# A decoder block's output projection: eight block products with all weights from one matrix, or seven with sums of blocks

## The chip, the core and the metric

The kernel runs on one core of a Trainium2 chip. The metric is the device time of one execution in microseconds, as the median of several runs. The engines are TensorE (PE, matmuls into PSUM banks of 128 x 512 fp32), VectorE (DVE) and ScalarE (ACT) for element-wise work, GpSimd (POOL), and SyncE (SP), whose queue issues nearly all DMAs here.

## What is computed

One decoder layer on 1024 tokens of width 1024, all in fp32. Cut to the part that matters:

```python
y_b = c @ w_proj_conv[l]                              # the conv projection
g_a, g_b = jnp.split(jax.nn.sigmoid(g + gate_b[l]), 2, axis=-1)
x = x + (g_a * y_a + g_b * y_b) @ w_out[l]            # the output projection
h = rms_norm(x, ffn_norm_w[l])
gt, up = jnp.split(h @ w_gate_up[l], 2, axis=-1)
x = x + (jax.nn.silu(gt) * up) @ w_down[l]
```

`m = g_a * y_a + g_b * y_b` is the 1024 x 1024 left matrix of the output projection, `w_out` the 1024 x 1024 right one.

## The kernel before

Every fp32 operand of a matmul is split into a high part (a cast to fp32r, `split_hi`, ScalarE, L119) and a low part (the difference, `split_lo`, VectorE, L124); a product is then three matmuls, hi x hi, hi x lo, lo x hi (`mm3`, L167). A weight tile of 128 x 1024 comes through a stream (`Stream`, L338): `next()` hands out the oldest tile and first fetches ahead until three are under way (load by SP into one of two buffers `wraw`, cast to `whi`, subtraction to `wlo`, three buffers each).

**Order of the work.** The instructions are traced in the order of the text. A scheduler then orders them on each engine by when it expects them to be ready; `with after(ins)` (L135) puts what is traced inside behind `ins` on that engine's queue. Each queue then runs strictly in its order.

**LayerNorm of the conv branch** (`ln_chunks`, L1519) works in two halves of 512 tokens (sb) during the attention projection, from a pool `b1` (`bp`), and fills `cT_hi`, `cT_lo`. Its last part runs into the conv projection.

**Conv projection** (L1633 to L1645). For each of 8 column blocks c of 128 channels and each half sb: 24 matmuls into one of four PSUM banks (`gemm_T`), the gate loaded (`gated`, L1597, four buffers `gt`), `ya` loaded (L1640), then on VectorE a product (L1642) and a sum (L1643), which give the block (c, sb) of m transposed, and a split into `mT_hi`, `mT_lo`. The blocks go in the groups (0,1,2), (3,4), (5,6), (7).

**Output projection** (L1701 to L1724). m is the stationary operand, w_out the moving one, 512 columns wide. Three passes (`WO`, L440): columns 0 to 511 for all eight token tiles (eight banks), then columns 512 to 1023 for tokens 0 to 511 (four banks), then for tokens 512 to 1023 (four banks). Per pass eight inner blocks k; a weight tile holds two of them (`ld_pair`, L425). Behind the first weight load SP loads the eight row tiles of x into `xa` (L1711), in the room that b1 left. After a pass VectorE adds each bank to `xa` (L1720), SP stores it to `x2_d` (L1721), ScalarE takes the sum of squares (`squares`, L1665).

**The FFN's norm.** When both column halves of tokens 0 to 511 are done, `rows_of` (L1669) computes 1/rms in 15 tiny VectorE operations (L1671, L648 to L660), `norm2` (L1674) scales a row tile (L1678), transposes it on TensorE (L1681) and splits it into `h2_hi`, `h2_lo`. Tokens 0 to 511 are turned in the third pass behind k = 3 to 6, in four banks that the pass does not use. The FFN's first gate product (`gate(0, 0)`, L1743) follows at once and takes a bank of the tag "pg" of the pool `ps`.

**Seven block products.** The FFN already uses Winograd's form of a 2 x 2 block product with 7 instead of 8 products. `SEVEN` (L447) lists left side, right side, bank ("a", "b" or "c", four PSUM banks each), result block and whether it is then complete. Left sides S1 to S4 and right sides T1 to T4 are sums of blocks; a bank is added to the result after each of its products and goes on accumulating. `ld_seven` (L457) loads a left and a right side (256 KB each) per step, `weight_sums` (L507) makes T1 to T4 of a weight matrix from loaded rows and stores them to DRAM in pieces of 128 KB, `side_sums` (L535) makes S1 to S4. In the down projection (`seven`, L482) both sides come from DRAM.

Of the kernel before, what the change touches and what calls it, by code (L numbers as in the profile page):

```python
# [10 lines left out]
F32 = mybir.dt.float32  # L11
# [5 lines left out]
P = 128  # L17
S = 1024
# [39 lines left out]
def kernel(  # L58
# [329 lines left out]
    td = {z: [dr.tile([P, 512], F32, name=f"td{z}_{j}") for j in range(NFF // 2)] for z in SUMS}  # L388
    b_d = dr.tile([H, TL], F32, name="b_d")
# [35 lines left out]
    def ld_pair(w, k, c):  # L425


        def go():
            raw = wraw()
            nc.sync.dma_start(  # L430
                raw[:].rearrange("p (k c) -> p k c", c=512),
                w[k * P : (k + 2) * P, 512 * c : 512 * (c + 1)].rearrange("(k p) c -> p k c", p=P),
            )
            hi, lo = wsplit(raw)
            return hi[:].rearrange("p (k c) -> p k c", c=512), lo[:].rearrange("p (k c) -> p k c", c=512)

        return go


    WO = ((0, (0, 1)), (1, (0,)), (1, (1,)))  # L440
    for c, _ in WO:
        ws.plan([ld_pair(wout, k, c) for k in range(0, NKT, 2)])

# [10 lines left out]
    def ld_seven(n, sides, w, sums, raw_tile):  # L457
# [22 lines left out]
        return [step(a_, b_, j) for a_, b_, _, _, _ in SEVEN for j in range(n)]  # L480

    def seven(n, stream, bank, add, soon):  # L482

        o = {}
        for z, (_, _, s_, (l, c), full) in enumerate(SEVEN):
# [3 lines left out]
            for js in [[j] for j in range(n - 2)] + ([[n - 2, n - 1]] if z == 6 else [[n - 2], [n - 1]]):  # L489
# [4 lines left out]
                for i in range(4):  # L494
# [9 lines left out]
                    if js[-1] == n - 1:  # L504
                        add(l, i, c, o[s_][i], full)

# [997 lines left out]
    bp = b1.enter_context(tc.tile_pool(name="b1", bufs=2, reuse_waits="tile"))  # L1504

# [13 lines left out]
    def ln_chunks(sb):  # L1519
# [4 lines left out]
        def half(tag):  # L1524
            return bp.tile([P, 512], F32, tag=tag, name=nm("ln" + tag), bufs=2)
# [8 lines left out]
        s1h, s1l = [bp.tile([P, 512], F32R, tag="sq", name=nm(t_), bufs=2) for t_ in ("lnmh", "lnml")]  # L1534
# [37 lines left out]
    part = bp.tile([P, P], F32R, tag="part", name="part", bufs=1)  # L1572
    pool.memset(f32(part[:]), 1.0 / D)

# [21 lines left out]

    def gated(d, cs):  # L1597
        g = bp.tile([P, 512], F32, tag="gt", name=nm("gt"), bufs=4)
        nc.sync.dma_start(g[:], d[:, cs])
        act.activation(g[:], g[:], AF.Sigmoid)  # L1600
        return g
# [30 lines left out]
    mT_hi, mT_lo = [a_[:5] + b_ + a_[5:] for a_, b_ in zip(y_first("mT"), y_last("mT"))]  # L1632
    for cl in ((0, 1, 2), (3, 4), (5, 6), (7,)):  # L1633
        pair = [(c, ws.next()) for c in cl]
        for sb in range(2):
            cs = slice(sb * 512, (sb + 1) * 512)
            for c, w in pair:
# [6 lines left out]
                split_hi(mT_hi[c][:, cs], g[:])  # L1644
                split_lo(mT_lo[c][:, cs], g[:], mT_hi[c][:, cs])  # L1645
# [12 lines left out]
    h2_hi = big.tile([P, NKT, S], F32R, tag="xhi", name="h2_hi")  # L1658
    h2_lo = big.tile([P, NKT, S], F32R, tag="xlo", name="h2_lo")
# [29 lines left out]
    wo_banks = [(ps, "pm"), (ps, "pm"), (ps, "pg"), (ps, "pg")] + [(pw, "pw")] * 4  # L1689

    def wo_bank(t_):
        p_, tag = wo_banks[t_]
        return p_.tile([P, 512], F32, tag=tag, name=nm("wo"))

    ntr = [0]

    def tr_first():
        ntr[0] += 1
        return ps.tile([P, 512], F32, tag=("pm", "pg")[ntr[0] % 2], name=nm("tr"))

    r2 = [None, None]  # L1701
    for z, (c, ls) in enumerate(WO):
        ts_ = [4 * l + i for l in ls for i in range(4)]
        o = {t_: wo_bank(t_) for t_ in ts_}
        for k in range(NKT):
            if k % 2 == 0:
                whi, wlo = ws.next()
            if z == 0 and k == 0:
                with after(last_of(mybir.EngineType.SP)):
                    for i in range(NT):  # L1710
                        nc.sync.dma_start(xa[i][:], xs[i * P : (i + 1) * P, :])  # L1711
            for t_ in ts_:
                tk = slice(t_ * P, (t_ + 1) * P)
# [278 lines left out]
```

## Time and profile before

| | us |
|---|---|
| median of 3 runs (lowest, highest) | 1742.43 (1741.9, 1744.05) |
| the profiled execution | 1742.87 |
| its span in the trace | 1741.1 |
| conv projection, TensorE | about 920 to 1008.5 |
| output projection, TensorE | 1008.5 to 1099.2 |

A page of the profile gives each engine's busy time, and the chain of work that ended last, followed back from the end. "L120" is a line of the kernel. Timelines list instructions with start, duration, engine, operation, tiles out<-in, and in brackets the idle time of the engine before and what ended it. A matmul's duration in the trace is longer than the distance to the next one, since matmuls are pipelined.

### The profile page before, as it was taken

The numbers are of one execution on the slowest core, as the hardware profiler recorded it, in microseconds if no ns is written. First come the engines' busy times: TensorE is split into PE (matmuls) and PEld (weight loads), VectorE is DVE, ScalarE is ACT, GpSimd is POOL, SyncE is SP. The second block draws the span as 40 slices with busy tenths as digits, with TensorE's granted clock in tenths as the row PEclk, the third lists the DMA queues.
The fourth block names the chain that finished last, engine by engine and source line by source line (L and its number), as shares of the span: only waits on it lengthen the run. The fifth ranks groups of instructions, "written<-read, shape, count | busy, mean of one in ns | idle before, by whom it ended". The sixth has DMA issues, their size and how long they took to land.

```text
span 1741.1 us, 25854 instructions
## 1 busy us (share of the span) xinstructions
PE 1728.2 (99%) x9293; PEld 1488.6 (85%) x9293; DVE 1249.4 (72%) x2090; ACT 856.2 (49%) x1950; POOL 210.9 (12%) x199
## 2 busy tenths in 40 slices
PE   9999999999999999999999999999999999999999
PEld 7997889998998999988787888888888888888887
DVE  7575889898987988977787525876676666565554
ACT  5333435767776776756366313633333333333332
POOL 3997851000000000000000000000000000000000
PEclk9999999999999999999999999999999999999999
DMA  6343454234345244343863544235445444597663
GB/s 200 118 129 119 161 177 140 91 107 134 104 110 151 80 119 131 103 140 135 310 208 100 173 157 154 89 99 185 152 152 173 160 151 147 173 369 274 216 219 130
DMA packets 253253, 271.68 MB, mean 156 GB/s; under 512 B 15746, under 2 KB 177602, under 8 KB 253124
## 3 DMA queue, kind: packets, MB, share of 16 engines
q1 hardware_dynamic: 250848, 263.25, 46.7%
q0 software_dynamic: 1840, 5.19, 1.0%
q8 instruction: 73, 1.20, 0.3%
q10 hardware_dynamic: 436, 1.58, 0.2%
q14 instruction: 56, 0.46, 0.1%
HBM read 175.55 MB, written 78.16 MB: 146 GB/s over the span
## 4 chain that ended last, share of the span: by engine, by line
PE 91%; DVE 3%; DMA 2%; ACT 2%; POOL 1%; issue 1%; SPq 0%; POOLq 0%; DVEq 0%
PE acc L963 28%; PE acc L500 12%; PE pg L168 11%; PE pg L170 11%; PE pg L169 11%; PE sc L1272 2%; PE sc L1271 2%; PE pT L1310 2%; PE wo L170 2%; PE wo L169 2%; PE wo L168 2%; DVE acc L582 1%; PE pW L169 1%; PE pW L168 1%; PE pW L170 1%; PE pg L1089 1%
## 5 line engine op out<-in xcount | busy, mean ns | idle before, releaser
L582 DVE SCALAR_TENSOR_TENSOR acc<-u,cw,acc 128x1023 f32<-128x1023 f32 (+14 forms) x240 | 303.5, 1265 | 14.4 <-ACT acc L576 11.9
L168 PE MATMUL pg<-whi,hT_hi 128*128 128x256 f32 x704 | 200.2, 286 | 0.5 <-DVE v L125 0.5
L170 PE MATMUL pg<-whi,hT_lo 128*128 128x256 f32 x704 | 200.1, 285 | 0.0
L169 PE MATMUL pg<-wlo,hT_hi 128*128 128x256 f32 x704 | 199.7, 284 | 0.0
L120 ACT CAST whi<-wraw 128x1024 fp32r<-128x1024 f32 x100 | 105.0, 1052 | 126.4 <-PE wo L170 48.2
L125 DVE TENSOR_TENSOR wlo<-draw,whi 128x1024 fp32r<-128x1024 f32 x75 | 91.8, 1224 | 86.1 <-ACT whi L120 84.4
L125 DVE TENSOR_TENSOR wlo<-wraw,whi 128x1024 fp32r<-128x1024 f32 x85 | 104.9, 1236 | 56.5 <-ACT whi L120 55.9
L120 ACT CAST whi<-draw 128x1024 fp32r<-128x1024 f32 x75 | 79.0, 1053 | 129.6 <-PE acc L500 116.1
L168 PEld LDWEIGHTS pg<-whi,hT_hi 128*128 128x128 f32 x704 | 134.1, 191 | 2.2 <-DVE v L125 0.7
L169 PEld LDWEIGHTS pg<-wlo,hT_hi 128*128 128x128 f32 x704 | 134.4, 191 | 1.9
L170 PEld LDWEIGHTS pg<-whi,hT_lo 128*128 128x128 f32 x704 | 134.3, 191 | 1.7
L500 PE MATMUL acc<-wlo,whi 128*128 128x512 f32 x308 | 120.0, 390 | 0.0
L500 PE MATMUL acc<-whi,wlo 128*128 128x512 f32 x308 | 119.9, 389 | 0.0
L168 PE MATMUL pg<-hT_hi,whi 128*128 128x512 f32 x288 | 114.7, 398 | 0.1
L169 PE MATMUL pg<-hT_lo,whi 128*128 128x512 f32 x288 | 114.2, 397 | 0.0
L170 PE MATMUL pg<-hT_hi,wlo 128*128 128x512 f32 x288 | 113.8, 395 | 0.0
L1278 ACT ACTIVATE E<-E,mn 128x640 f32<-128x640 f32 (+7 forms) x128 | 99.7, 779 | 27.1 <-DVE mn L1273 26.4
L120 ACT CAST whi<-s 128x1024 fp32r<-128x1024 f32 x54 | 56.9, 1053 | 107.3 <-PE acc L963 103.5
L963 PE MATMUL acc<-h_hi,whi 128*128 128x512 f32 x240 | 93.5, 390 | 0.0
L963 PE MATMUL acc<-h_lo,whi 128*128 128x512 f32 x240 | 93.5, 390 | 0.0
L1273 DVE CUSTOM_DVE_ANT_0 E<-sc,tb 128x512 f32<-128x512 f32 (+3 forms) x128 | 74.1, 585 | 26.9 <-PE pT L1310 13.1
L963 PE MATMUL acc<-h_hi,wlo 128*128 128x512 f32 x240 | 90.2, 390 | 0.0
(337 smaller groups left out, 4554.9 us busy)
## 6 DMA issues: line engine op xcount, KB each, us to landing
wraw<-in_w_gate_up_dram SPq DMA_DIRECT2D x44, 512.0 KB, 4.9
wraw<-in_w_in_dram SPq DMA_DIRECT2D x40, 512.0 KB, 4.6
qs<-qs SPq DMA_DIRECT2D x96, 128.0 KB, 2.3
wd<-in_w_down_dram SPq DMA_DIRECT2D x44, 256.0 KB, 3.1
tdT<-wd SPq DMA_DIRECT2D x88, 128.0 KB, 4.7
draw<-sdS SPq DMA_DIRECT2D x44, 256.0 KB, 3.7
draw<-tdT SPq DMA_DIRECT2D x44, 256.0 KB, 4.0
wraw<-in_w_in_dram SPq DMA_DIRECT2D x32, 256.0 KB, 3.3
```

The lines of the kernel that those rows point to most:

```text
L120: act.copy(dst, src)
L125: last_lo[0] = dve.tensor_tensor(dst, src, f32(hi), op=ALU.subtract).ins
L168: pe.matmul(o, lh, rh, start=start, stop=False)
L169: pe.matmul(o, lh, rl, start=False, stop=False)
L170: last_mm[0] = pe.matmul(o, ll, rh, start=False, stop=stop).ins
L500: m = pe.matmul(o[s_][i][:], l_[:, ts], r_[:, 512:], start=start and j + y_ == 0, stop=j == n - 1 and y_ == 2, skip_group_check=not start,)
L582: dve.scalar_tensor_tensor(a_, us[c][:, : S - n], cw[:, c, t : t + 1], a_, op0=ALU.mult, op1=ALU.add)
L963: last_mm[0] = pe.matmul(o[:], a_[x_][:, k, :], b_[y_][:, k, :], start=start and k + x_ + y_ == 0, stop=k == 3 and x_ == 1, skip_group_che ...
L1271: pe.matmul(o[:, :w], qh[:, qs], k, start=True, stop=False)
L1272: last_mm[0] = pe.matmul(o[:, :w], ql[:, qs], k, start=False, stop=True).ins
L1273: dve.tensor_tensor_reduce(e[:, ks], o[:, :w], tb[:, S - nk + c0 : S - nk + c0 + w], 1.0, mn[:, j : j + 1] if c0 else 3.0e38, ALU.add, ALU ...
L1278: act.activation(e[:, :nk], e[:, :nk], AF.Exp, bias=mn[:, j : j + 1], scale=-1.0, accum_out=l[:, j : j + 1])
```

## The change

The output projection becomes seven block products. m is cut into 2 x 2 blocks of 512 tokens x 512 channels, where the channel blocks are those of even and odd c, so that a pair (c - 1, c) gives one piece of every block; w_out is cut likewise, its row tiles into even and odd ones.

- Right sums: `weight_sums` of w_out, 8 chunks, one after every second of the 16 turns of the conv projection, queued behind VectorE's last instruction there; stored to `to` in DRAM.
- Left sums: after both halves of a pair, `side_sums` makes S1 to S4 from the four unsplit blocks and stores them to `so`. The unsplit blocks stay in `gt` buffers until then; a second set of four buffers is added in a pool `bs`, in the room of the LayerNorm's tiles, which get a pool of their own that closes before the conv projection.
- The left blocks 11, 12 and 22 are read from `mT_hi`, `mT_lo` in place; for even c the second token half is no longer split.
- Order of the products (`WSEVEN`): 11 (bank b), 12 (a), S2 (b), S1 (c), S4 (c), S3 (b), 22 (b). Weight steps: two tiles of two pairs for 11, 12 and 22 (`ld_two`), four tiles (left | right) for each S.
- Loads of S2, S1 and S4 with their right sides go into 12 rooms of 128 x 1024, in the place of `cT_hi` and half of `cT_lo`; SP gets them in one block behind the last load: S2, four row tiles of x, S1, four row tiles of x, S4. S3 goes through the two `wraw` buffers.
- After each product VectorE adds its four banks to `xa`, complete or not. The transposes of `norm2` take the banks of a and c; they are traced behind step 3 of S3 and steps 0 to 2 of 22.

```diff
+    so = {z: [dr.tile([P, 512], F32, name=f"so{z}_{j}") for j in range(NKT // 2)] for z in SIDES[3:]}
+    to = {z: [dr.tile([P, 512], F32, name=f"to{z}_{j}") for j in range(NKT // 2)] for z in SUMS}
...
-    for c, _ in WO:
-        ws.plan([ld_pair(wout, k, c) for k in range(0, NKT, 2)])
+    WSEVEN = tuple(SEVEN[z] for z in (0, 1, 2, 3, 5, 4, 6))
...
+    for e_ in WSEVEN:
+        if e_[0][0] == "S":
+            wo_steps[e_[0]] = ld_seven(NKT // 2, so, wout, to, wo_raw, (e_,))
+        else:
+            wo_steps[e_[0]] = [ld_two(e_[1], q) for q in range(2)]
+        ws.plan(wo_steps[e_[0]])
...
+    osum = weight_sums(NKT // 2, wout, to, wo_tiles, 256)
+    osum[0][0]()
...
                 dve.tensor_tensor(g[:], g[:], ya[:], op=ALU.add)
-                split_hi(mT_hi[c][:, cs], g[:])
-                split_lo(mT_lo[c][:, cs], g[:], mT_hi[c][:, cs])
+                if c % 2 or not sb:
+                    split_hi(mT_hi[c][:, cs], g[:])
+                    split_lo(mT_lo[c][:, cs], g[:], mT_hi[c][:, cs])
+                M[c, sb] = g
+                if c % 2 and sb:
+                    s1, s3 = [bs.tile([P, 512], F32, tag=t_, name=nm(t_), bufs=1) for t_ in ("s1", "s3")]
+                    side_sums(
+                        *[M.pop(k_) for k_ in ((c - 1, 0), (c - 1, 1), (c, 0), (c, 1))],
+                        s1, {z: so[z][c // 2][:] for z in so}, s3,
+                    )
+                nturn += 1
+                if nturn % 2 == 0:
+                    with after(last_of(mybir.EngineType.DVE)):
+                        if len(osum) > 1:
+                            osum[1][0]()
+                        osum.pop(0)[1]()
...
+    for z, (z_, b_, s_, (l, c), full) in enumerate(WSEVEN):
+        start = s_ not in o
+        if start:
+            o[s_] = [p_.tile([P, 512], F32, tag=tag, name=nm("wo")) for p_, tag in wo_banks[s_]]
+        for j in range(4):
+            if z_[0] == "S" or j % 2 == 0:
+                hi, lo = ws.next()
+            if z == 0 and j == 0:
+                with after(last_of(mybir.EngineType.SP)):
+                    for step in wo_steps["S2"]:
+                        step.load()
+                    x_rows(0)
+                    for step in wo_steps["S1"]:
+                        step.load()
+                    x_rows(1)
+                    for step in wo_steps["S4"]:
+                        step.load()
...
+            if 0 <= 4 * (z - 5) + j - 3 < 4:
+                with after(last_mm[0]):
+                    norm2(4 * (z - 5) + j - 3, r2[0], tr_first)
+        for i in range(4):
+            t_ = 4 * l + i
             h = xa[t_][:, TOK[c]]
-            dve.tensor_tensor(h, o[t_][:], h, op=ALU.add)
-            nc.sync.dma_start(x2_d[t_][:, TOK[c]], h)
-            squares(t_, c)
+            dve.tensor_tensor(h, o[s_][i][:], h, op=ALU.add)
+            if full:
+                nc.sync.dma_start(x2_d[t_][:, TOK[c]], h)
+                squares(t_, c)
```

More of the change, by code (lines that the diff above doesn't have):

```diff
@@ L478, in step @@
             return go
[L480 removed]
+        return [step(a_, b_, j) for a_, b_, _, _, _ in which for j in range(n)]
     def seven(n, stream, bank, add, soon):
@@ L1504 @@
     bp = b1.enter_context(tc.tile_pool(name="b1", bufs=2, reuse_waits="tile"))
+    part = bp.tile([P, P], F32R, tag="part", name="part", bufs=1)
+    pool.memset(f32(part[:]), 1.0 / D)
     for h in (5, 6):
```

107 lines of the change are left out of this document (64 added, 43 removed).

## The prediction

> **What bounds the kernel now.** First the page's head: spans by engine, and the chain of work that ended last.
>
> ```profile
> span 1741.1 us, 25854 instructions
> PE 1728.2 (99%) x9293; PEld 1488.6 (85%) x9293; DVE 1249.4 (72%) x2090; ACT 856.2 (49%) x1950; POOL 210.9 (12%) x199
> ...
> PE 91%; DVE 3%; DMA 2%; ACT 2%; POOL 1%; issue 1%; SPq 0%; POOLq 0%; DVEq 0%
> ```
>
> TensorE is idle for 12.9 us of the whole span, and 91% of the chain is its own. A matmul less is time less, as long as the stage it leaves stays without gaps. So I ask for the stages that the change touches: engine time by stretch (columns: length, busy time and instructions of PE, PEld, DVE, ACT, POOL; granted clock; DMA share; GB/s).
>
> ```profile
> 840.00:850.00 10.00, 6.67 (x28) 4.75 (x26) 7.35 (x11) 5.14 (x7) 0.00 (x0) 0.98 0.72 264
> 850.00:860.00 10.00, 9.94 (x38) 8.11 (x39) 9.68 (x17) 2.10 (x4) 0.00 (x0) 0.85 0.94 322
> 920.00:960.00 40.00, 39.59 (x172) 31.62 (x171) 30.79 (x47) 24.41 (x39) 0.00 (x0) 1.00 0.31 103
> 960.00:1008.50 48.50, 48.50 (x215) 40.19 (x214) 24.27 (x32) 15.19 (x24) 0.00 (x0) 1.00 0.44 148
> 1074.00:1099.20 25.20, 25.20 (x129) 21.16 (x128) 19.27 (x39) 14.36 (x28) 0.00 (x0) 1.00 0.39 124
> 1540.00:1560.00 20.00, 20.00 (x90) 16.58 (x89) 14.90 (x19) 7.38 (x7) 0.00 (x0) 1.00 1.04 375
> ```
>
> The conv projection (920 to 1008.5) and the output projection (to 1099.2) keep TensorE full but for 0.4 us. VectorE is the one to watch: three quarters full in both 920 to 960 and 1074 to 1099.2.
>
> **What is removed.** The output projection's matmuls, from the view of its tile, then from TensorE's timeline at its two ends, and the transposes in it from the chain of work:
>
> ```profile
> L168 PE MATMUL wo<-whi,mTh x128: 388/390/482, 1008.5 to 1098.5; 128*128 128x512 f32 x128
> ```
> ```profile
> 1008.51 0.39 PE L168 MATMUL wo<-whi,mTh 128*128 128x512 f32 x1
> ...
> 1099.16 0.39 PE L168 MATMUL pg<-h_hi,whi 128*128 128x512 f32 x1
> ```
> ```profile
> 1085.06 0.87 PE tr L1681 x8
> ```
>
> Three lines of 128 make 384 matmuls. One lasts 0.39 us but the next starts long before its end, so the price is the spacing: 1099.16 - 1008.51 = 90.65 us, less 32 transposes (four times 0.87 = 3.5 us), over 384 = **0.227 us**. Seven products of 4 pairs x 4 token tiles x 3 matmuls are 336. The 48 that go save 48 x 0.227 = **10.9 us**; the transposes stay. This is the most that there is to gain. A product is 48 x 0.227 = 10.9 us long, a step of one pair 2.72 us.
>
> **What is added, and where it lies.** *Splits.* 22 weight tiles are cast and subtracted instead of 12. The down projection already runs this rhythm; ScalarE's and VectorE's timelines there:
>
> ```profile
> 1587.55 1.06 ACT L120 CAST whi<-draw 128x1024 fp32r<-128x1024 f32 x1 [1.67 <-PE acc L500]
> 1590.27 1.05 ACT L120 CAST whi<-draw 128x1024 fp32r<-128x1024 f32 x1 [1.66 <-PE acc L500]
> ```
> ```profile
> 1568.02 0.42 DVE L525 TENSOR_TENSOR wd<-wd 128x256 f32<-128x256 f32 x1
> ...
> 1587.06 2.48 DVE L1935 TENSOR_TENSOR xr<-acc,xr 128x512 f32<-128x512 f32 x4
> 1589.45 1.22 DVE L125 TENSOR_TENSOR wlo<-draw,whi 128x1024 fp32r<-128x1024 f32 x1
> ```
>
> One tile per 2.72 us, cast 1.05 and subtraction 1.22 us, four adds between, and TensorE full. With three buffers a cast starts two steps (5.44 us) ahead of need, so a split has 5.44 - 1.05 - 1.22 = 3.2 us to spare. Ten more splits cost nothing under that cover; if VectorE is held longer than 3.2 us, the rest is a gap.
>
> *Sums in the conv projection.* Eight chunks of four 128x256 operations (4 x 0.42 = 1.7 us, 13.4 in all), four side sums of four 128x512 operations (0.69 each, 2.8 us, 11.0 in all), less four low halves not made (2.8): VectorE goes from 55.1 to about 77 of 88.5 us. In 920 to 960, with the rest of the LayerNorm, 30.8 become 38 to 40 of 40 (three chunks 5.0, one or two side sums 2.8 to 5.5, one or two low halves less). Here VectorE already ends last once (TensorE's timeline):
>
> ```profile
> 955.77 0.50 PE L170 MATMUL pg<-cT_hi,wlo 128*128 128x512 f32 x1 [0.40 <-DVE wlo L125]
> ```
>
> If a chunk or a side sum is queued ahead of that low half, it is added to the 0.4: 0 to 4.5 us. A gain is excluded, since nothing leaves VectorE there before it. Four accumulator banks let TensorE run ahead elsewhere. Value nearest to half a chunk: **+0.8**.
>
> *Transfers.* The stage's own bytes, from the DMA view over 920 to 1008:
>
> ```profile
> DMA packets 9116, 11.29 MB, mean 128 GB/s; under 512 B 560, under 2 KB 4656, under 8 KB 9110
> ```
>
> Added: w_out read once (4.2 MB), four weight sums and four side sums written (4.2 each): 23.9 MB in 88.5 us, 270 GB/s. The stretch 1540 to 1560 moved 375 GB/s with TensorE full, in the same sorts of transfer, of which the page's list of issues has (KB each, us to landing):
>
> ```profile
> tdT<-wd SPq DMA_DIRECT2D x88, 128.0 KB, 4.7
> draw<-sdS SPq DMA_DIRECT2D x44, 256.0 KB, 3.7
> ```
>
> So I charge nothing. The Trainium skill speaks against such small pieces: DMA: Bandwidth & Descriptors, section Bandwidth, asks for transfers of 1 MiB for three quarters of the peak and lists 138 GB/s at 64 KB; by an estimate from that page's 138 GB/s the stage would last 173 us. The 375 GB/s row, with 128 and 256 KB transfers in flight together, disagrees.
>
> *The start of the output projection.* Behind the conv projection SP gets 32 loads, 10.5 MB: sums for S2, S1, S4 and the rows of x. SP's timeline shows that its order is not that of the text, and the list of issues how long rows of x take in a burst:
>
> ```profile
> 857.00 0.42 SPq L1640 DMA_DIRECT2D ya<-ya_d  x1
> ...
> 859.65 0.47 SPq L1546 DMA_DIRECT2D cT_lo<-lnd  x1
> ```
> ```profile
> xa<-in_x_dram SPq DMA_DIRECT2D x8, 512.0 KB, 9.0
> ```
>
> L1640 belongs to the conv projection, yet stands before LayerNorm stores written earlier: what is expected to be ready goes first. Rows of x wait for the room of the last sums (after the last matmul four operations on the block, 2.8, its side sums 2.8, the last chunk 1.7, a store 4.7: 12 us), so loads of S2, S1 and S4 will pass them. Ahead of the first four rows' landing stand 5.8 to 8.9 MB, at 375 GB/s 15.5 to 23.8 us. New: the first product's adds need these rows, since its bank is written again by S2 at 2 x 10.9 = 21.8 us; behind the adds in VectorE's queue wait the low half of S2's first weights (1.2 us). Late by 0 to 2, with adds 2.5 and the low half 1.2: 0 to 5.7 us. Value **+1.5**, nearer to the early end, because part of the first x rows' room is free before 12 us.
>
> *Banks taken over at once.* S4 follows S1 in bank c, 22 follows S3 in bank b. TensorE returns to a tile after nine matmuls (2.04 us); the add needs 0.16 (the matmul's own end) + 0.69. 1.2 us to spare, which one split of 1.22 uses up: 0 to 1.2 each, **+0.6** together.
>
> *Norm beside splits.* VectorE and ScalarE in the last group of before:
>
> ```profile
> 1071.95 2.73 DVE L1720 TENSOR_TENSOR xa<-wo,xa 128x512 f32<-128x512 f32 x4 [1.09 <-PE wo L170]
> ...
> 1076.35 0.16 DVE L1671 TENSOR_TENSOR ssq<-ssq,ssq 128x4 f32<-128x4 f32 x1
> ...
> 1079.08 5.39 DVE L1678 SCALAR_TENSOR_TENSOR xa<-xa,r,fnw_b 128x512 f32<-128x512 f32 x8
> 1084.38 1.22 DVE L125 TENSOR_TENSOR wlo<-wraw,whi 128x1024 fp32r<-128x1024 f32 x1
> ...
> 1098.25 0.68 DVE L125 TENSOR_TENSOR h_lo<-tr,h_hi 128x512 fp32r<-128x512 f32 x1
> 1098.85 1.88 DVE L1720 TENSOR_TENSOR xa<-wo,xa 128x512 f32<-128x512 f32 x3
> ```
> ```profile
> 1079.43 1.06 ACT L120 CAST whi<-wraw 128x1024 fp32r<-128x1024 f32 x1 [3.11 <-PE wo L170]
> ```
>
> The cast ended at 1080.49, its subtraction ran at 1084.38: 3.9 us behind eight scalings. Before, a weight tile served 5.44 us and this was harmless. Now the same scalings fall into S3, at 2.72 us a tile with 3.2 us to spare: 0.7 late plus hand-overs. 0 to 3.9, **+1.2**.
>
> *The gate's bank.* The first FFN product takes a "pg" bank. Before, transposes held it; now tile 2 of product 22 does, until its add. The third of the four adds above ended near 1100.1, TensorE wanted the bank at 1099.16: 0.25 (no low half between) to 1.6, **+1.0**.
>
> SP and POOL: SP issues some 64 more transfers in the conv projection, about 0.4 us each, 26 of 88 us; POOL gets only one memset earlier. The residual adds grow from 16 to 28 (8 us on VectorE), already in the terms above.
>
> **Sum.** -10.9 + 0.8 + 1.5 + 0.6 + 1.2 + 1.0 = -5.8 us. The profiled execution took 1742.87 us (span 1741.1); it becomes 1737.1. The median of the runs, 1742.43, lies 0.44 lower: **1736.6 us**.
>
> **Rivals.**
> *All hidden.* VectorE's order happens to suit, x rows land by 20 us: only the bank of the gate is left, 1742.4 - 10.9 + 0.3 = about 1732. For it: 1540 to 1560 is full at the same pace. Against: the 3.9 us. 0.15.
> *Gain eaten.* Two or three of the terms reach their upper ends (5.7 at S2, 3.9 at S3): another 3 to 9 us, 1739 to 1746, about 1742. For it: a full VectorE at 920 to 960 and in S3. 0.20.
> *Slower: x rows last.* SP puts the rows behind all loads that are ready sooner. 10.5 MB and 1.6 MB of last stores at 375 GB/s are 32 us; adds and low half to 36: TensorE stands 14 us at S2, once. After a gap the clock drops: 3.3 us of idling in 840 to 850 left a granted 0.85 in the next 10, 1.5 us lost. -10.9 + 14 + 1.5 + 3.6 = +8: about 1751. It passes zero when the rows land some 4 us past 21.8, and 3.5 us of loss when they land 7 past. Against: x stands second in the text and half of its room is free early. 0.15. The clock gate's page of the Trainium skill (TensorE: Matmul & The Clock Gate, section Part 1) has half rate after an idle window of about 3.4 us; by that only this rival pays, and the trace's 0.85 agrees.
>
> **Chances.** Forecast 0.50 (1733 to 1739). A measurement of this kernel tells about 0.2%, 3.5 us, from no change. Below 1738.9: forecast and all-hidden, 0.63. Within: most of "eaten", 0.21. Above 1745.9: 0.16. The range 1731.4 to 1746 leaves out the slower rival.
>
> **What would show it.** 336 matmuls of the projection, spaced 0.227. TensorE's waits name VectorE's adds or low halves: S2's first step (x rows' landing after 20 us), S3's third step, the first gate matmul behind an add. If the waits in 920 to 1100 are under 1 us together, all-hidden holds; if the conv projection itself is longer than 88.5 us, my transfer or VectorE terms are wrong; a granted clock under 1 after 1030 tells the slower rival.

## The result, and the profile after

The changed kernel takes **1754.8 us** (median of 4 runs, 1752.71 to 1757.04), the kernel before 1742.8 in the same session (1741.9 to 1744.05): a ratio of 1.0069, 95% interval 1.0051 to 1.0086. It is slower by 12 us. The forecast was 1736.6 and faster; both its sign and its range (to 1746.0) are wrong. Ratios leave disturbed executions out (one of run 4, of 3478.87 us) and so can differ a little from the quotient of two medians. Times are medians, while the tables by stage and the lines come from one profiled execution of each kernel, and single executions lie up to some 5 us from their median (run 4: 1742.7 to 1750.8; the profiled one of run 2 took 1743.76 for a median of 1739.6).

The page's head and the chain that ended last, of the changed kernel:

```profile
span 1754.7 us, 26010 instructions
PE 1726.1 (98%) x9245; PEld 1482.7 (84%) x9245; DVE 1284.9 (73%) x2156; ACT 864.1 (49%) x1956; POOL 210.7 (12%) x199
...
PE 85%; DVE 6%; DMA 5%; ACT 2%; issue 1%; SPq 0%; DVEq 0%; ACTq 0%
```

The 48 matmuls are gone (9245 for 9293 records), yet TensorE's busy time fell by 2.1 us only (half clock took the rest, see below), and its idle time rose from 12.9 to 28.6 us. Of the chain, DMA now has 5% where it had 2%, and VectorE 6% where it had 3%. TensorE's waits between 900 and 1150 us (columns: what waited, for what, us in total, times, longest), largest first:

```profile
PE wo L1776 <- DVE xa L1786: 4.7, 2, 4.4
PE wo L1776 <- DVE gt L1674: 3.9, 1, 3.9
PE tr L1725 <- ACT xa L1730: 1.6, 2, 1.3
PE pg L170 <- DVE wlo L125: 1.5, 1, 1.5
PE pg L168 <- ACT whi L120: 1.4, 1, 1.4
PE pg L168 <- ACT h_hi L120: 0.8, 1, 0.8
PE wo L1776 <- DVE r L671: 0.7, 1, 0.7
PE pg L169 <- DVE h_lo L125: 0.4, 1, 0.4
```

Before, the one wait of the conv projection was 0.4 us. The same stretch by windows (columns as in the prediction's table: length, five engines, granted clock, DMA share, GB/s):

```profile
840.00:860.00 20.00, 16.89 (x60) 12.77 (x59) 17.15 (x25) 7.03 (x10) 0.00 (x0) 0.83 0.86 304
960.00:1000.00 40.00, 40.00 (x178) 33.14 (x177) 26.84 (x46) 10.24 (x16) 0.00 (x0) 1.00 0.93 300
1000.00:1020.00 20.00, 18.33 (x81) 14.83 (x80) 13.07 (x22) 3.33 (x5) 0.00 (x0) 1.00 0.64 192
1020.00:1040.00 20.00, 17.81 (x71) 14.60 (x72) 10.81 (x15) 5.53 (x7) 0.00 (x0) 0.91 1.02 348
1040.00:1060.00 20.00, 15.64 (x57) 12.10 (x57) 10.87 (x15) 6.87 (x13) 0.00 (x0) 0.83 1.04 409
...
1100.00:1120.00 20.00, 17.24 (x82) 13.50 (x81) 19.35 (x40) 14.55 (x28) 0.00 (x0) 0.91 0.58 181
```

Two things are new here. The DMA engines are full where they were 0.44 busy, at 300 GB/s in the conv projection. And the granted clock is below 1 in three windows behind 1000 us, where it was 1.00 throughout before: 20 x 0.09, 20 x 0.17 and 20 x 0.09 are 1.8, 3.4 and 1.8 us of TensorE's time, 7 us together. The first row, in the LayerNorm, has 20 x 0.17 = 3.4 us of the same kind; before, its two halves (0.98 and 0.85 of 10 us) lost 1.7. TensorE's waits there are the same in both kernels (1.8 and 1.0 us, for the LayerNorm's mean), so a longer stretch at half clock behind the same waits is 1.7 of the 1.8 us by which the conv projection begins later below.

**The first gap.** SP's longest waits from 1000 to 1020 us, then three engines' timelines around the last turn of the conv projection, SP, ACT, TensorE:

```profile
SPq L533 <- DMA toT<-wd: 4.5, 1, 4.5
SPq L1619 <- DMA soS<-gt: 4.2, 1, 4.2
```
```profile
1011.41 0.94 SPq L558 DMA_DIRECT2D soS<-gt  x2
1016.55 0.32 SPq L1619 DMA_DIRECT2D gt<-g_d  x1
```
```profile
1019.68 0.63 ACT L1620 ACTIVATE gt<-gt 128x512 f32<-128x512 f32 x1 [13.82 <-DMA gt<-g_d]
```
```profile
1022.19 0.50 PE L1776 MATMUL wo<-whi,mTh 128*128 128x512 f32 x1 [3.86 <-DVE gt L1674]
...
1024.27 0.63 PE L1776 MATMUL wo<-whi,mTh 128*128 128x512 f32 x1
1024.69 0.63 PE L1776 MATMUL wo<-wlo,mTh 128*128 128x512 f32 x1
```

S2 and S4 are made in place, in two of the gate's buffers, and stored from there at 1011.41. The load of the last gate input needs such a buffer; SP issues it only at 1016.55, when the first of those stores has landed, and stands until then with all that is behind it. ScalarE waits 13.82 us for the input, the last turns' multiply (L1674), which frees their accumulator banks, comes late, and the first product, which needs these banks, stands 3.86 us. The wait of 4.2 us is the second of two in a row: just before, SP stood 4.5 us at the load of the next right-sum chunk (L533, issued at 1008.49), since a store of the chunk before still held its buffer. VectorE had finished S2 and S4 by 1007.9; their stores left at 1011.41. Behind the gap the matmuls are 0.43 us apart (1024.27, 1024.69) instead of 0.227: half clock.

**The second gap**, at S2; SP, VectorE, TensorE:

```profile
1036.98 6.68 SPq L1744 DMA_DIRECT2D xa<-in_x_dram  x8
```
```profile
1043.44 0.69 DVE L1732 TENSOR_SCALAR fnw_b<-fnw_b 128x1024 f32<-128x1024 f32 x1 [4.26 <-DMA fnw_b<-in_ffn_norm_w_dram]
1044.17 0.69 DVE L1786 TENSOR_TENSOR xa<-wo,xa 128x512 f32<-128x512 f32 x1
```
```profile
1045.01 0.77 PE L1776 MATMUL wo<-whi 128*128 128x512 f32 x1 [4.36 <-DVE xa L1786]
```

All eight rows of x go out in one go, behind all 16 loads of S2 and S1 and the first three of S4. SP's largest waits at the rows (1030 to 1046 us) are for landings of such loads, whose data the rows don't need:

```profile
SPq L1744 <- DMA room<-toT: 2.1, 3, 0.9
SPq L1744 <- DMA room<-soS: 1.6, 3, 0.8
```

The trace's semaphores tell why. The transfers that SP and ScalarE issue go round eight semaphores, and an issue waits until the transfer eight before it has landed: no more than eight are under way. Between 1020 and 1045 us 22 of 36 issues follow such a landing within 0.15 us. The first row landed at 1044.05, and the first add began at 1044.17.

The first product began at 1012.96, so S2 was due 21.8 us later, at 1034.8; it began at 1045.01, 32.0 us later. The delay of 10.2 is the first gap with its half clock and this wait of 4.36.

**The norm's end**, TensorE:

```profile
1106.29 1.63 PE L1725 MATMUL tr<-ident,xa 128*128 128x128 f32 x12 [0.27 <-ACT xa L1730]
1109.23 0.66 PE L1725 MATMUL tr<-ident,xa 128*128 128x128 f32 x4 [1.32 <-ACT xa L1730]
1110.69 0.73 PE L168 MATMUL pg<-h_hi,whi 128*128 128x512 f32 x2 [0.80 <-ACT h_hi L120]
```

The transposes wait for banks that ScalarE still copies from, the gate's first product for its split. Before, the gate began with no gap.

By stages, from the first matmul of each (us of the span; all later tables are made in this way; "due" is 21.8):

| run | conv projection begins | its length | output projection | S2 behind its start | rest from the gate | span |
|---|---|---|---|---|---|---|
| before | 920.1 | 88.4 | 90.7 | none | 641.9 | 1741.1 |
| after | 921.9 | 91.0 | 97.7 | 32.0 | 644.0 | 1754.7 |

The output projection's matmuls need 90.65 - 10.9 = 79.8; it took 97.7. So the account of the 13.6 us of span is -10.9 for the matmuls, +1.8 ahead of the conv projection, +2.6 in it, +17.9 in the output projection and +2.1 behind the gate (1.8 of it half clock).

### The profile page after: what moved, and what is told of

It reads as the page before. It is cut to its first block, busy times and chain, and to the rows that moved or that the text cites. A ratio compares the mean times of both kernels' runs of the same rounds, so it can differ in the third digit from the quotient of the medians.

```text
span 1754.7 us, 26010 instructions
## 1 busy us (share of the span) xinstructions
PE 1726.1 (98%) x9245; PEld 1482.7 (84%) x9245; DVE 1284.9 (73%) x2156; ACT 864.1 (49%) x1956; POOL 210.7 (12%) x199
## 4 chain that ended last, share of the span: by engine, by line
PE 85%; DVE 6%; DMA 5%; ACT 2%; issue 1%; SPq 0%; DVEq 0%; ACTq 0%
PE acc L977 29%; PE acc L482 12%; PE pg L168 10%; PE pg L169 10%; PE pg L170 10%; PE sc L1286 2%; PE sc L1285 2%; PE wo L1776 2%; PE pT L1324 2%; DVE acc L596 1%; PE pW L169 1%; PE pW L168 1%; PE pW L170 1%; DMA soS<-gt 1%; PE pg L1103 1%
## 5 line engine op out<-in xcount | busy, mean ns | idle before, releaser
L125 DVE TENSOR_TENSOR wlo<-draw,whi 128x1024 fp32r<-128x1024 f32 x75 | 91.8, 1223 | 84.1 <-ACT whi L120 76.5
```

The source lines that it names most:

```text
L125: last_lo[0] = dve.tensor_tensor(dst, src, f32(hi), op=ALU.subtract).ins
```

## The experiments

Four theories were tried. *Buffers*: the sums made in place hold gate buffers. *Right sums*: their 8 MB of traffic, or their 13.4 us on VectorE, delay what the last turns and S2 wait for. *Hand-over*: the order at S2 (the norm weight's scaling ahead of the adds, x rows last) is the cost. *Addresses*: moving the LayerNorm's tiles into a pool of their own costs by itself. Where a run leaves out or changes part of the computation, its expectation or the text says which part. Ratios are to the kernel before.

**1. The LayerNorm pool alone**, put into the kernel before.

```
+    ln_ctx = ExitStack()
+    lp = ln_ctx.enter_context(tc.tile_pool(name="lnp", bufs=2, reuse_waits="tile"))
...
-            return bp.tile([P, 512], F32, tag=tag, name=nm("ln" + tag), bufs=2)
+            return lp.tile([P, 512], F32, tag=tag, name=nm("ln" + tag), bufs=2)
```

> The kernel before with one part of the change alone: the LayerNorm's tiles in a pool of their own, gate tiles ahead of them. The changed kernel starts its conv projection 1.8 us later than before (921.9 against 920.1). If the new addresses of these tiles cause that, this kernel is about 1744.5 us; if the 1.8 us come from elsewhere (the conv projection's loads, or the phase of the clock gate), it stays at 1742.8 within 1 us.

Measured: 1745.44 us (before 1743.21), ratio 1.0011 (1.0001 to 1.0021), nearer to the first case's number. TensorE's wait in the conv projection, which is 91.7 us long instead of 88.4, and the granted clock soon behind it (the wait ends at 956.63):

```profile
PE pg L168 <- DVE gt L1646: 2.0, 1, 2.0
```
```profile
958.00:961.00 3.00, 3.00 (x7) 1.99 (x8) 3.00 (x4) 0.62 (x1) 0.00 (x0) 0.50 0.50 150
```

So the move alone, without sums or products, costs 2.2 us. The changed kernel has other waits in that stage (1.4 and 1.5 us, for a weight tile), so how much of its loss this is stays open. Why tiles at other places delay a gate input, by their room or by the order that the queues get from it, was not separated.

**2. No right sums.** The T blocks are read as raw blocks of w_out: no loads, sums or stores for them.

```
-    osum = weight_sums(NKT // 2, wout, to, wo_tiles, 256)
...
+    RAW = {"T1": (0, 1), "T2": (0, 0), "T3": (1, 0), "T4": (1, 1)}
+    WSEVEN = tuple((e_[0], RAW.get(e_[1], e_[1])) + e_[2:] for e_ in [SEVEN[z] for z in (0, 1, 2, 3, 5, 4, 6)])
```

> The changed kernel without the sums of w_out: neither their loads (4.2 MB), their 32 VectorE operations (13.4 us) nor their stores (4.2 MB); the products read plain blocks of w_out in their place, so that part of the computation is left out. Theory A (gate buffers are held by the stores of the left sums S2 and S4, so gates come late): these stores remain, about 1751 us. Theory B (the volume of transfers, DMA share 0.93 to 1.04): two thirds of the added volume go, the gaps of 3.9 and 4.4 us with their half clock go, about 1743. Theory C (VectorE is full): about 1743 as well.

Measured: 1739.6 us, ratio 0.9983 (0.9974 to 0.9993): 15 us less than the changed kernel and below all three theories' numbers. S2 starts 21.7 us behind the first product, on time. TensorE's largest waits from 900 to 1150 us:

```profile
PE tr L1718 <- ACT xa L1723: 2.3, 2, 2.0
PE pg L168 <- DVE gt L1673: 1.5, 1, 1.5
PE wo L1769 <- DVE r L672: 1.5, 1, 1.5
...
```

Both large gaps are gone with the right sums, though S2 and S4 are still made and stored in the gate's buffers. SP stands at the last gate input's load here too, for 3.8 us, but issues it at 1005.12, 6.8 us ahead of the first product (changed kernel: 3.6 us behind its start): the hold costs TensorE only when the right sums' transfers have made SP late already.

**3. Left sums not stored**: made on VectorE, but S is fetched from rows that lie in memory from an earlier stage (other data, same size).

```
+    so = {z: [ya_d[2 * j + n % 2][:, 512 * (n // 2) : 512 * (n // 2 + 1)] for j in range(NKT // 2)] for n, z in enumerate(SIDES[3:])}
```

> The changed kernel with the left sums computed but not stored (4.2 MB of stores less); S1 to S4 are fetched from rows of ya instead, so the result leaves the true sums out. Theory A: the gate buffers come free at once, the gap of 3.9 us at the first product goes and the one at S2 shrinks, 1744 to 1746. Theory B: a third of the added volume goes, about 1750. Theory C: VectorE does the same work, 1754.

Measured: 1745.44 us, ratio 1.001 (1.0001 to 1.002), 9.4 less than the changed kernel, as theory A (*buffers*) had it. The first gap is gone, S2 starts 25.0 behind; the waits for its adds:

```profile
PE wo L1777 <- DVE xa L1787: 3.5, 2, 3.1
```

**4. S2 and S4 in tiles of their own.** Everything is computed.

```
+                    s2, s4 = [wp.tile([P, 512], F32, tag="sg", name=nm(t_), bufs=2) for t_ in ("s2", "s4")]
...
+                    dve.tensor_tensor(s2[:], s1[:], a11[:], op=ALU.subtract)
+                    dve.tensor_tensor(s4[:], a12[:], s2[:], op=ALU.subtract)
```

> The changed kernel with S2 and S4 written to two tiles of their own instead of the gate buffers; all transfers and all VectorE work stay. Theory A: the gate buffers come free right behind the sums, 1745 us. Theories B and C: nothing changes, 1754.

Measured: 1748.01 us, ratio 1.0021 (1.0012 to 1.0031), 6.8 less than the changed kernel (8 by the two ratios), and 3 above theory A's number. The 3.86 us gap and its half clock went; the work and the bytes are the same, only the order of the stores of sums moved a little. *Buffers* is shown, at 6.8 us beside the right sums' transfers. The second gap stayed; VectorE of this run:

```profile
1035.41 0.69 DVE L1737 TENSOR_SCALAR fnw_b<-fnw_b 128x1024 f32<-128x1024 f32 x1 [3.78 <-DMA fnw_b<-in_ffn_norm_w_dram]
1036.11 0.69 DVE L1791 TENSOR_TENSOR xa<-wo,xa 128x512 f32<-128x512 f32 x1
```

**5. The right sums on VectorE only**: made at their places from tiles of zeros, with no loads and stores.

```
-                        osum.pop(0)[1]()
+                        vsum(nturn // 2)
```

> The kernel after, with the right sums still made on VectorE at the same places (32 differences on two tiles of zeros), but without their loads and stores; the T blocks are read as raw blocks of the weights, so that the output is not the projection. It splits what went away with the right sums as a whole (1739.6 us against 1754.8). If the traffic of 8 MB costs the time (gate inputs and x rows come later through a full set of DMA engines), this run stays near 1740 (1738 to 1743), with the second product starting within 23 us of the projection's start. If it is the VectorE work in the conv projection, it stays at 1750 to 1755 with waits on gt and xa as in the kernel after.

Measured: 1739.59 us, ratio 0.9977 (0.9966 to 0.9987), the same as without any right sums. VectorE's part costs nothing: its conv projection is 88.7 us long. It is the loads and stores, by their bytes or by their places in SP's queue.

**6. The right sums 70 us earlier**, during the Y products, on GpSimd, from run 4 on. Everything is computed.

```
+    osum = weight_sums(NKT // 2, wout, to, wo_tiles, 256, pool)
...
+        for _ in range(2 if c < 4 else 1):
+            if len(osum) > 1:
+                osum[1][0]()
+            osum.pop(0)[1]()
```

> The kernel with S2 and S4 in tiles of their own (1748.0), and the right sums made during the Y products, 70 us earlier, on GpSimd in the ya buffers; everything is computed. If the traffic and its time are what costs, the second product starts on time (within 23 us of the projection's start) and the time is 1738 to 1743. If the sums cost wherever they are made (GpSimd or the DMA disturb the LN, which is on the edge there), the loss moves to the Y products: these or the conv projection grow by 3 us or more, and the time stays at 1745 to 1750.

Measured: 1743.97 us, ratio 0.9999 (0.999 to 1.0009). The time lies between the two theories' numbers. S2 is on time (21.7), the output projection 85.2 us long. But the conv projection grew to 94.1. TensorE's waits in this run, of those behind 900 us the three of the conv projection:

```profile
PE pg L168 <- ACT whi L120: 1.4, 1, 1.4
PE pg L170 <- DVE wlo L125: 1.2, 1, 1.2
...
PE pg L168 <- ACT cT_hi L120: 1.0, 1, 1.0
```

and its windows in the Y products, the conv projection, and around S2:

```profile
860.00:920.00 60.00, 60.00 (x276) 49.89 (x275) 49.90 (x89) 34.88 (x56) 22.77 (x24) 1.00 0.91 301
960.00:1000.00 40.00, 40.00 (x178) 33.14 (x177) 24.26 (x36) 11.93 (x18) 0.00 (x0) 1.00 0.62 207
1020.00:1040.00 20.00, 20.00 (x90) 16.56 (x89) 9.77 (x12) 6.71 (x12) 0.00 (x0) 1.00 1.02 387
```

The last row matters: around S2 the DMA engines are as full as in the changed kernel (1.02, 387 GB/s), and S2 has no wait. So full DMA engines by themselves don't make S2 late. The rival's loss by moving held: the LayerNorm's rows share 860 to 920 with the sums, and it ends late.

**7 and 8. The hand-over mended**, on run 6 and on run 4: the norm's weight fetched and scaled later, rooms for S3's loads.

```
+        if z == 2:
+            nc.scalar.dma_start(wb2[:], ffn_norm_w.to_broadcast([P, D]))
+        if z == 3:
+            dve.tensor_scalar(wb2[:], wb2[:], -0.125, None, op0=ALU.mult)
```

> The run with early right sums, and besides: the norm's weight is fetched behind the third product and scaled behind the fourth, and the loads of S3 have rooms of their own instead of two streaming buffers. Everything is computed. By the theory that the hand-over at S2 and the two buffers at S3 cost 3 to 6 us with their half-clock stretches, this run is 3 us below the run with early right sums alone, 1734 to 1739, and faster than both kernels. If the scaling ahead of the additions was only the last of several late events, it is within 1.5 us of that run.

> The kernel with S2 and S4 in tiles of their own (1748.0), with only the hand-over mended (norm's weight later, rooms for S3), the right sums left in the conv projection. If the order of the hand-over costs the time, 1743 to 1745, with S2 starting at most 23 us behind the projection's start. If the x rows are late because the DMA engines are full (15.6 MB in the 45 us around), S2 still starts 24 us or more behind, and the time is 1746 to 1748.

Measured: 1744.21 us, ratio 1.0004 (0.9995 to 1.0014), and 1749.07, ratio 1.003 (1.0019 to 1.0041): nothing gained on either, and in both the gate's first product now waits 2.5 us for its split instead of 0.8. In run 8, S2 starts 26.6 us behind and now waits 4.6 us for the adds themselves. The scaling that stood ahead of them in the profile was only the last of several late events; *hand-over* as an order on VectorE falls.

**9 and 10. Half of the right sums early, half in the conv projection's middle**, on GpSimd, and the low parts of the gate's first weights there too; run 10 also moves the low parts of the LayerNorm's second half.

```
+        if c > 3:
+            if c < 7:
+                osum[1][0]()
+            osum.pop(0)[1]()
...
+                low_by_pool[0] = z == 6
```

> The kernel with S2 and S4 in tiles of their own (1748.0), the right sums on GpSimd and spread over the stretch where the DMA engines are least busy: four chunks during the last four Y products, four in the conv projection's middle turns, none in its last five; and the low parts of the gate's first weights split off on GpSimd. Everything is computed. By the theory that only bytes in the wrong 60 us cost, the conv projection loses at most 3 us (early sums at full rate cost it 5.6), S2 starts on time, the norm's end loses 2 us less, and the time is 1736 to 1740, below both kernels. By the rival, that the LN's end is disturbed by any change around it, the conv projection loses 4 us or more and the time is 1741 to 1745.

> The run before this one, and besides the low parts of the LN's second half made on GpSimd (1.3 us each instead of 0.7). If VectorE is what makes the LN's end late in the conv projection, that stage is 1 to 3 us shorter than in the run before and the time falls by as much. If the LN's end is a chain of latencies through ACT and DVE, it is the same within 1 us, or 1 us longer since the last low part takes 0.6 us more.

Measured: 1751.16 us, ratio 1.0043 (1.0029 to 1.0057), and 1752.27, ratio 1.005 (1.0037 to 1.0062). Run 9 missed both theories' numbers; run 10 is 1.1 us longer than run 9, as its second case said. S2 is on time in both (21.7, 21.8), but the conv projection takes 97.3 and 97.0 us; its largest wait in run 9:

```profile
PE pg L168 <- ACT cT_hi L120: 3.0, 2, 2.7
```

The LayerNorm's end comes later with four chunks beside it than with eight in run 6; why is open. Run 10 shows that the low parts on VectorE aren't what holds it. The norm's end, which was to lose 2 us less, got worse: the gate's first product waits 2.2 and 3.0 us for its split, where run 6 waited 0.8.

**11. The traffic alone, in the kernel before**: w_out loaded and stored in eight portions through GpSimd's queue, nothing computed from it.

```
+                            pool.dma_start(
+                                t_[:].rearrange("p (h c) -> p h c", c=256),
+                                wout[r0 : r0 + P, :].rearrange("p (h c) -> p h c", c=512)[:, :, q : q + 256],
+                            )
+                            for n_, z in enumerate((("T1", "T3"), ("T4", "T2"))[e]):
+                                pool.dma_start(to[z][j][:, q : q + 256], t_[:, 256 * n_ : 256 * (n_ + 1)])
```

> The kernel before, with the traffic of the right sums alone put into its conv projection: the weight blocks are loaded (4 MB) and stored (4 MB) in eight portions on GpSimd's queue, nothing is computed from them and nothing reads them. By the theory that it is the sum of the traffic behind the gate inputs and ahead of the x rows that costs, and not 8 MB alone, this run is within 2 us of the kernel before (1743 to 1745): its conv projection uses under half of the DMA engines' time. If traffic of this size costs by itself (the last gate inputs or the x rows come later), it is 4 us or more slower.

Measured: 1745.18 us, ratio 1.001 (1.0001 to 1.0019), as the theory expected. The place isn't the one meant: GpSimd had nothing to wait for and most of it went at 860 to 900.

```profile
860.00:900.00 40.00, 40.00 (x184) 33.23 (x183) 31.71 (x59) 21.67 (x34) 13.14 (x22) 1.00 0.96 335
960.00:1000.00 40.00, 40.00 (x178) 33.12 (x177) 21.10 (x29) 14.47 (x22) 0.00 (x0) 1.00 0.53 172
```

TensorE stays full beside DMA engines that are 0.96 busy. 8 MB cost 1.9 us where nobody waits for what is queued with them. Since queue, kernel and most of the time differ, this is no test of the same bytes in SP's queue at 960 to 1035 us.

**12. The right sums in the first stage** (70 to 270 us), on VectorE. Everything is computed.

```
+        if 14 <= n < 38:
+            k, e = divmod(n - 14, 3)
+            if e < 2:
+                with after(last_of(mybir.EngineType.DVE)):
+                    osum[k][e]()
```

> The kernel with S2 and S4 in tiles of their own (1748.0), and the right sums made long before, between 70 and 270 us of the span, on VectorE, in two tiles that stand empty there; the DMA engines are busy for 0.34 to 0.52 of that time and VectorE for 0.4 to 0.9. Everything is computed, nothing of the right sums is left in the 200 us around the projection. By the theory that the sums cost only where their traffic meets the LN's rows, the gate inputs, the left sums and the x rows, the conv projection loses at most 3 us, S2 starts within 23 us of the projection's start, and the time is 1737 to 1741, below both kernels. If it is 1743 or more, a loss that has nothing to do with the right sums (the LN's end, the norm's end, the left sums) is larger than the runs without right sums showed.

Measured: 1772.31 us, ratio 1.0173 (1.0159 to 1.0188). Around the projection it went as expected: S2 on time, conv projection and output projection together 176.0 us (before 179.0). But the conv projection begins at 950.5, 30 us late, 27 of them lost by the start of the attention, where the sums were put. TensorE's waits there (100 to 270 us), then one sum on VectorE and GpSimd's work beside it:

```profile
PE acc L977 <- DVE u L1010: 7.6, 3, 3.9
PE acc L977 <- POOL wlo L131: 5.4, 2, 3.3
```
```profile
196.78 1.25 DVE L596 SCALAR_TENSOR_TENSOR acc<-u,cw,acc 128x1001 f32<-128x1001 f32 x1
197.95 7.79 DVE L542 TENSOR_TENSOR wd<-wd 128x256 f32<-128x256 f32 x1
205.66 0.68 DVE L1012 TENSOR_TENSOR u<-acc,u 128x512 f32<-128x512 f32 x1
```
```profile
197.04 1.28 POOL L960 TENSOR_TENSOR s<-wraw,wraw 128x512 f32<-128x512 f32 x1
...
203.06 2.39 POOL L131 TENSOR_TENSOR wlo<-s,whi 128x1024 fp32r<-128x1024 f32 x1
```

A subtraction of 0.42 us took 7.79, as long as GpSimd's five operations beside it (197.04 to 205.45).

**13. The right sums at the end of the attention**, in the background queue behind the convolution's taps. Everything is computed.

```
+    for k in range(0, 8, 2):
+        bg.add([osum[k][0], osum[k + 1][0], osum[k][1], osum[k + 1][1]])
```

> The kernel with S2 and S4 in tiles of their own (1748.0), with the right sums behind the convolution's last taps, in the background queue that fills VectorE's slack in the attention, in the convolution's empty input tiles. Everything is computed. By the theory that the price of the right sums is that of the place, and that the attention has room (VectorE 0.86, DMA 0.40 busy), the stretch from the start of the conv projection to the first gate is 175 to 177 us as in the run with the sums in the first stage (before: 179.0), the attention is at most 1 us longer, and the time is 1738 to 1741, below both kernels. If VectorE's slack is all used, the attention grows by 5 to 10 us, and the time is 1745 to 1750.

Measured: 1749.56 us, ratio 1.0037 (1.0024 to 1.005). From the conv projection to the gate 174.9 us, the shortest of all; S2 on time. But the conv projection begins 10.4 us late: the attention's end had no room for them. The rival's number held.

**14. Half of the x rows and S4's blocks written behind the start of S2**, on run 4.

```
+            if z == 2 and j == 0:
+                with after(last_mm[0]):
+                    x_rows(1)
```

> The kernel with S2 and S4 in tiles of their own (1748.0), with the rows 4 to 7 of x and the blocks of S4 fetched only from the start of the second product's matmuls on (3.5 MB that nobody needs earlier). Everything is computed. If it is what is fetched ahead of the first x rows in those 20 us that makes the second product late, S2 starts within 23 us of the projection's start (25.2 in the run without this edit), a stretch at half clock goes with the wait, and the time is 1743 to 1745. If the first x rows wait for their room in SBUF or for the left sums, S2 starts 24 us or more behind, and the time is 1747 to 1750, or more if rows 4 to 7 are now late for S1.

Measured: 1748.06 us, ratio 1.0026 (1.0017 to 1.0036). Inconclusive: SP's order is not that of the text, and all eight rows still went out together:

```profile
1029.77 6.79 SPq L1749 DMA_DIRECT2D xa<-in_x_dram  x8
```

So the question behind it, what the x rows wait for, was not tried by this run; the traces below answer it.

The runs beside each other. "Last store of sums" and "first x row" are when these have been issued, in us behind the first matmul of the output projection; "ahead" is how many transfers SP and ScalarE issue from that matmul up to the first row:

| run | conv projection | S2 (due 21.8) | output projection | last store of sums | first x row | ahead | time, us |
|---|---|---|---|---|---|---|---|
| after | 91.0 | 32.0 | 97.7 | 18.5, right | 24.0 | 35 | 1754.8 |
| 3 left sums not stored | 92.8 | 25.0 | 89.3 | 11.2, right | 17.0 | 26 | 1745.4 |
| 4 own tiles | 90.6 | 25.2 | 90.7 | 12.1, right | 17.6 | 29 | 1748.0 |
| 8 hand-over alone | 90.6 | 26.6 | 92.4 | 13.0, right | 18.5 | 31 | 1749.1 |
| 2 no right sums | 89.1 | 21.7 | 86.1 | 7.5, left | 14.5 | 22 | 1739.6 |
| 5 VectorE only | 88.7 | 22.3 | 87.0 | 7.9, left | 15.0 | 22 | 1739.6 |
| 6 sums early | 94.1 | 21.7 | 85.2 | 7.1, left | 10.7 | 16 | 1744.0 |
| 12 first stage | 91.2 | 21.8 | 84.8 | 7.1, left | 10.0 | 16 | 1772.3 |
| 13 attention | 90.8 | 21.8 | 84.1 | 7.3, left | 10.7 | 16 | 1749.6 |

S2 is on time whenever the last store in front is one of left sums, and late whenever it is one of right sums. In all nine traces the first row of x goes out within 0.15 us of the landing of the transfer eight before it; it is issued at 0.60 to 0.69 us for each transfer ahead. So the place in the queue decides, not room in SBUF: 22 transfers ahead are still in time (21.7 and 22.3), 26 aren't. The row lands 6 to 7 us later, and in the late runs the first add follows at once (after: issued at 24.0, add at 31.2; run 4: 17.6 and 24.3). Not tried: x rows ahead of the loads of S1, right sums stored through another queue, or in fewer and larger pieces. The last two would tell the price of a place in the queue from that of bytes, since around S2 the DMA engines are full (1.02 to 1.04).

## Why the prediction was wrong

*The gain* was right. The matmuls still come 0.227 us apart at full clock, and in runs 12 and 13 S2 starts 21.8 us behind the first product, two products' time as worked out.

*"So I charge nothing"* for the transfers is the step that failed. The 375 GB/s row was read as a rate that leaves room above 270 GB/s. What counted was what is queued behind each transfer. SP's 64 more transfers were priced at 0.4 us of issuing each; in the trace SP stands at a load until its buffer's store has landed (4.5 and 4.2 us), and at any transfer until the one eight before it has landed. Taking the loads and stores of the right sums away, and leaving their VectorE work, gave back 15.2 us (run 5), while as many bytes cost 1.9 us on GpSimd's queue, where nobody waits (run 11). The rate was also too high for this stretch: 300 GB/s took 0.93 of the DMA engines, so about 320 is all of it, by an estimate from those two numbers. The Trainium skill (DMA: Bandwidth & Descriptors, section Bandwidth), weighed there with an estimate of 173 us for the stage, isn't borne out either: the stage took 91.0.

*The buffers* were not foreseen at all. The prediction asked whether VectorE had time for the sums, not that an in-place sum holds its buffer until the store has landed, and that the next gate input waits for it with all of SP's queue. It costs 6.8 us (run 4), of which 3.86 is the gap.

*The hand-over, +1.5 (0 to 5.7)*, had the right event, x rows behind the last sums, with another cause and too small a size. Its 12 us run to the landing of the last store, which frees the rows' room; that store landed at 16.0 in run 4 and at 22.5 in the changed kernel (issued at 12.1 and 18.5). But the rows didn't wait for room: they stood in SP's queue behind 35 transfers, eight under way at a time (why the scheduler put them there, no run shows), and all eight went together at 24.0, where the prediction let some go early, "because part of the first x rows' room is free before 12 us". S2 was 10.2 us late for an allowed 0 to 2. The *slower* rival, at 0.15, was the nearest to what came: 1751 against 1754.8, by the rows that it names, though with two smaller gaps in place of one of 14 us.

*The clock*: "only this rival pays" was wrong. Gaps of 3.86 and 4.36 us paid 1.8 and 3.4 us, the norm's end 1.8. The rule of the Trainium skill (TensorE: Matmul & The Clock Gate, section Part 1), half rate behind an idle window of about 3.4 us, agrees with the first two but is too generous: in run 1 a single gap of 1.99 us and in run 3 one of 3.09 us were followed by 3.4 us at half clock. The gate's three pauses are each shorter still (0.27, 1.32, 0.80 us, with transposes between), and run 13 has the same pauses within 0.3 us and a granted clock of 1.00 there:

```profile
1100.00:1120.00 20.00, 17.44 (x86) 13.68 (x85) 17.96 (x38) 13.52 (x27) 0.00 (x0) 1.00 0.50 153
```

*Sums in the conv projection, +0.8 (0 to 4.5)*: the stage grew by 2.6, within the bounds, but not by the sums on VectorE: with all of them there and no traffic it is 88.7 us long (run 5). TensorE's two waits in it, 1.4 us for the high and 1.5 for the low part of a weight tile, also stand in runs 6 and 12, which have no right sums there (1.4 and 1.2), and what makes them is open. The move of the LayerNorm's tiles, which got no term at all, makes the stage 91.7 alone (run 1), but runs 2 and 5, which have the move too, take 89.1 and 88.7.

*Banks +0.6, norm +1.2*: waits of 0.3 for an add and 0.7 for the norm's factors; right, or a little high. *The gate's bank +1.0*: not the bank but the transposes' banks and the split, 1.6 + 0.8 + 0.4, and half clock on top.

*Can the change pay?* Without the right sums' traffic it gains 3.7 us of the 10.9 (run 5, not the whole computation); the rest goes to the conv projection's edge, the norm's end and its half clock. With everything computed no version here beats the kernel before: the best is run 6 at 0.9999, no change. In each place that was tried the right sums cost at least that gain.

## What to carry to other kernels

When a transform moves operands through memory, follow each new store to whoever waits for its buffer and each new load to what stands ahead of it in its queue, up to the first matmul that needs the result; a free share of bandwidth says little on that. Here each transfer ahead in the queue was worth 0.6 to 0.7 us. Make sums that are to be stored in tiles of their own, not in the buffers of a running stream. A gap of 4 us on a TensorE-bound path should be counted at 6 to 8, with its stretch at half clock.

## What the runs showed of the hardware

Two-operand subtractions on VectorE between SBUF tiles, 0.42 us in the conv projection, took 0.97, 1.31, 0.92 and 1.70 us on average in the first stage of run 12 (eight of each), up to 7.79, while GpSimd ran two-operand operations; convolution taps (1.25 us) and additions that read a PSUM bank (0.68) kept their times beside it. The Trainium skill (SBUF — State Buffer, section SBUF: two separate sides) describes the port pair that VectorE and GpSimd share as an exclusive lock, whose loser waits for the whole instruction; the 7.79 us beside five GpSimd operations agree, and show that the loser may wait for several in a row.

The rate at which the DMA engines are full differed between two stretches of one run: 300 GB/s at a share of 0.93 in the conv projection, 409 at 1.04 around S2.

In the clock records of these traces nearly every stretch at half clock ahead of the last matmuls lasts 3.41 or 6.83 us, whatever the gap: 3.41 behind single gaps of 1.99 (run 1), 3.09 (run 3) and 3.86 us (changed kernel), 6.83 behind 3.2 (run 4), 4.36 (changed kernel) and 4.6 us (run 8). One, in run 9, lasts 10.24.
